# One product of seven made by seven smaller ones, for two sets of output features at a time

## The chip, the core and the metric

The kernel runs on one core of a Trainium2 chip. The core has a matrix engine (TensorE, PE in the profile, with its weight loads as PEld), a vector engine (VectorE, DVE), a scalar engine (ScalarE, ACT), a general engine (GpSimd, POOL) and a queue engine that issues most transfers (SyncE, SP). Each runs its own list of instructions in order, and they wait for one another by semaphores. The metric is the device time of one execution in microseconds (us). Before the change it is 1542.12 us, the median of 3 runs (1541.8 to 1542.74).

## What is computed

One layer for 1024 prompt tokens and 32 sample tokens, together 1056 columns, with 1024 features:

```python
proj = rmsnorm(x, g_mix) @ w_in              # 1024 -> 5120
q, k, v, cb, cc, cx, ga, gc = split(proj)    # 512 each, the gates 1024 each
y_attn = attend(q, k, v) @ w_attn_out
y_conv = (cb * causal_conv(cc * cx)) @ w_conv_out
x = x + (sigmoid(ga) * y_attn + sigmoid(gc) * y_conv) @ w_o
x = x + square(relu(rmsnorm(x, g_ffn) @ w_up)) @ w_down
x = x + sigmoid(rmsnorm(x, g_ple) @ w_ple_gate) * (p @ w_ple)
```

All of it is in fp32. A product of matrices is made in three passes over rounded parts (high by high, high by low, low by high), so each block of weights and activations exists as a high part, rounded by ACT, and a low part, subtracted by DVE.

## The kernel before

Features lie on the partitions, tokens along the columns. The input stage (`w_in`) and the up stage (`w_up`) go set by set: a set is two blocks of 128 output features. `seven` (L206) makes a set by Winograd's form of Strassen's scheme: the set's weights are four quarters (two output blocks by the even and the odd four of the eight blocks of input features), the activations four quarters B11 to B22 (even and odd features by two halves of the tokens), and seven products of sums replace eight. Each product is made in two pieces of 264 columns, and each piece is 12 matmuls (4 blocks of features, three passes). The order on PE is A11·B11, S1·T1, S2·T2, A12·B21, S3·T3, S4·B22, A22·T4, each as piece 0 and piece 1. S2, S3 and A22 add into the same accumulators as A11 (`x`), S4 into that of S1 (`z`), after ACT or DVE has read the earlier sum out (L227 to L256).

PE's list is written by hand. `run` (L268) advances the body of a set by one step, which is mostly one piece, and after it every generator in `side` by one step: `prepare` (L168) makes the weights of the next set (four sums on POOL, then casts on ACT and subtractions on DVE), `fetch_in` and `fetch_up` load the set after it, and `follow` (L575) works on the outputs of the set just made: for q and k a scaling and a split, for v a shift difference `dv` and transposes, for cc, cx and cb the convolution (`conv_in`, L535: scale, multiply, two passes with the taps). `stats_x` (L396) finds the norms of the rows, and PE spreads them by small matmuls over `dg` tiles (L384). So what ACT, DVE and POOL do, and in which order, follows from the step in which it is written.

In the up stage `up_set` applies relu and square on ACT as the sums come out, and `mid_sums` (L1257) makes four sums of halves on DVE for the down stage.

## Time and profile before

| what | us |
|---|---|
| median of 3 runs | 1542.12 |
| the profiled execution | 1543.23 |
| its span, first to last instruction | 1541.5 |
| TensorE busy in the span | 1520.1 |
| VectorE busy | 1061.1 |
| ScalarE busy | 756.8 |
| GpSimd busy | 347.1 |

The busy time of PE is the union of its instructions, which overlap: a matmul is recorded for longer than the distance to the next. What a matmul costs is read from a stretch without gaps, as its length over its count. Waits are listed by the engine that waited and the one that ended the wait.

### The profile page before, as it was taken

The page shows a single profiled execution, that of the slowest core. Times are in us where ns is not written, and L with a number is a line of the kernel's source. Part 1 is how long each engine was busy: PE and PEld are TensorE (multiplying, and loading weights), DVE is VectorE, ACT ScalarE, POOL GpSimd, SP SyncE. Part 2 cuts the span into 40 slices and gives each one's busy share as a digit, 9 for nine tenths or more (in the row PEclk, how much of TensorE's full clock was granted, in tenths as well). Part 3 has the DMA queues.
Part 4 walks back from the last instruction along what each step waited for, and adds up shares of the span by engine and source line. Part 5 has one row for each costly group of instructions (what it writes and reads, how often), then busy time and mean ns, then how long its engine had stood idle before and what let it go on. Part 6 is the DMA issues. An engine that isn't in the chain of part 4 may idle for free.

```text
span 1541.5 us, 29349 instructions
## 1 busy us (share of the span) xinstructions
PE 1520.1 (99%) x11786; PEld 1506.4 (98%) x11786; DVE 1061.1 (69%) x1394; ACT 756.8 (49%) x1384; POOL 347.1 (23%) x294
## 2 busy tenths in 40 slices
PE   8999999999999999999999999999999999999997
PEld 8999999999999999999999999999999999999997
DVE  7534786666688887766677555554586986789856
ACT  6543344443566774333355555555534334444656
POOL 1122332220211105002312222221020221012453
PEclk9999999999999999999999999999999999999999
DMA  6532145544735566235454334434886897583443
GB/s 235 185 123 69 45 178 204 197 146 111 218 108 152 177 220 243 87 125 182 166 184 148 139 141 153 144 136 147 290 305 203 281 327 250 188 283 106 144 132 111
DMA packets 111559, 269.10 MB, mean 175 GB/s; under 512 B 13472, under 2 KB 29216, under 8 KB 111424
## 3 DMA queue, kind: packets, MB, share of 16 engines
q1 hardware_dynamic: 110704, 265.05, 50.9%
q8 instruction: 92, 1.51, 0.4%
q10 hardware_dynamic: 720, 2.19, 0.4%
q14 instruction: 43, 0.35, 0.1%
HBM read 186.46 MB, written 80.73 MB: 173 GB/s over the span
## 4 chain that ended last, share of the span: by engine, by line
PE 92%; DVE 4%; ACT 2%; issue 1%; DMA 0%; SPq 0%; POOL 0%; DVEq 0%; ACTq 0%; POOLq 0%
PE ps_dn L1473 7%; PE ps_dn L1472 7%; PE ps_dn L1474 7%; PE ps_A11u L203 4%; PE ps_A11u L202 4%; PE ps_A11u L204 4%; PE ps_A11i L202 4%; PE ps_A11i L204 4%; PE ps_A11i L203 4%; PE av L874 2%; PE ps_wo L106 2%; PE ps_wo L107 2%; PE ps_wo L108 2%; PE ps_S1u L203 2%; PE ps_S1u L202 2%; PE ps_S1u L204 2%
## 5 line engine op out<-in xcount | busy, mean ns | idle before, releaser
L1473 PE MATMUL ps_dn<-fl,whi_dn 128*128 128x264 f32 x896 | 255.0, 285 | 0.1
L1474 PE MATMUL ps_dn<-fh,wlo_dn 128*128 128x264 f32 x896 | 255.1, 285 | 0.0
L1472 PE MATMUL ps_dn<-fh,whi_dn 128*128 128x264 f32 x896 | 254.9, 285 | 0.0
L1473 PEld LDWEIGHTS ps_dn<-fl,whi_dn 128*128 128x128 f32 x896 | 168.6, 188 | 0.3 <-DVE fl L1381 0.3
L1472 PEld LDWEIGHTS ps_dn<-fh,whi_dn 128*128 128x128 f32 x896 | 168.7, 188 | 0.0
L1474 PEld LDWEIGHTS ps_dn<-fh,wlo_dn 128*128 128x128 f32 x896 | 168.6, 188 | 0.0
L189 POOL TENSOR_TENSOR s_i<-raw_i,raw_i 128x512 f32<-128x512 f32 x30 | 40.5, 1348 | 227.8 <-DVE slS_i L152 206.7
L1365 DVE TENSOR_TENSOR wlo_dn<-raw_dn,whi_dn 128x1024 fp32r<-128x1024 f32 x40 | 71.1, 1778 | 25.1 <-ACT whi_dn L1359 24.4
L819 DVE TENSOR_TENSOR_SCAN r<-r 128x128 f32<-128x128 f32 (+3 forms) x64 | 86.6, 1355 | 2.1 <-POOL r L812 2.1
L1359 ACT CAST whi_dn<-raw_dn 128x1024 fp32r<-128x1024 f32 x40 | 42.0, 1051 | 93.7 <-PE ps_dn L1473 79.5
L189 POOL TENSOR_TENSOR s_u<-raw_u,raw_u 128x512 f32<-128x512 f32 x30 | 44.2, 1473 | 186.1 <-DVE slS_u L152 157.4
L1414 POOL TENSOR_TENSOR c<-c,rs 128x528 f32<-128x528 f32 x16 | 26.7, 1669 | 244.2 <-DVE c L1481 122.7
L1381 DVE TENSOR_TENSOR fl<-mr,fh 128x1056 fp32r<-128x1056 f32 x56 | 69.8, 1248 | 4.6 <-ACT fh L1376 4.6
L152 DVE TENSOR_TENSOR slS_i<-s_i,shS_i 128x512 fp32r<-128x512 f32 x45 | 36.0, 802 | 49.2 <-ACT shS_i L150 49.0
L202 PE MATMUL ps_A11i<-T,shS_i 128*128 128x264 f32 x240 | 68.6, 286 | 0.2 <-ACT u_i L235 0.2
L202 PE MATMUL ps_A11u<-T,shS_u 128*128 128x264 f32 x240 | 68.5, 285 | 0.0
L203 PE MATMUL ps_A11u<-T,shS_u 128*128 128x264 f32 x240 | 68.4, 285 | 0.0
L203 PE MATMUL ps_A11i<-T,shS_i 128*128 128x264 f32 x240 | 68.2, 284 | 0.0
L204 PE MATMUL ps_A11i<-T,slS_i 128*128 128x264 f32 x240 | 68.2, 284 | 0.0
L204 PE MATMUL ps_A11u<-T,slS_u 128*128 128x264 f32 x240 | 68.2, 284 | 0.0
L812 POOL TENSOR_SCALAR_AFFINE_SELECT r<-r 128x128 f32<-128x128 f32 x64 | 26.3, 412 | 166.1 <-ACT r L805 166.0
L1376 ACT CAST fh<-mr 128x1056 fp32r<-128x1056 f32 x56 | 60.1, 1073 | 5.5 <-DMA mr<-mdB 5.5
(462 smaller groups left out, 5594.7 us busy)
## 6 DMA issues: line engine op xcount, KB each, us to landing
raw_dn<-in_w_down_dram SPq DMA_DIRECT2D x56, 512.0 KB, 4.5
raw_i<-in_w_in_dram SPq DMA_DIRECT2D x34, 512.0 KB, 4.4
mr<-mdT SPq DMA_DIRECT2D x32, 528.0 KB, 5.4
raw_u<-in_w_up_dram SPq DMA_DIRECT2D x32, 512.0 KB, 3.6
mdB<-m SPq DMA_DIRECT2D x48, 264.0 KB, 2.5
mr<-mdB SPq DMA_DIRECT2D x24, 528.0 KB, 6.4
s<-gd SPq DMA_DIRECT2D x16, 528.0 KB, 5.4
mdT<-ta SPq DMA_DIRECT2D x32, 264.0 KB, 2.1
```

The lines of the kernel that those rows point to most:

```text
L189: f()
L202: nc.tensor.matmul(p_, wh[:, k, :], o[:, 0, c], start=new and n == 0, stop=False, **on)
L203: nc.tensor.matmul(p_, wh[:, k, :], o[:, 1, c], start=False, stop=False, **on)
L204: nc.tensor.matmul(p_, wl[:, k, :], o[:, 0, c], start=False, stop=z, **on)
L819: nc.vector.tensor_tensor_scan(rev, rev, rev, 1.0, ALU.mult, ALU.bypass)
L1359: nc.scalar.copy(hi, dws[u])
L1365: dve(lo, raw, hi.bitcast(F32), op=sub)
L1376: nc.scalar.copy(h, mraw[v])
L1381: dve(l, mraw.pop(v), opd[v].bitcast(F32), op=sub)
L1472: nc.tensor.matmul(ps, hi[:, j, :], oh, start=j == 0, stop=False)
L1473: nc.tensor.matmul(ps, hi[:, j, :], ol, start=False, stop=False)
L1474: nc.tensor.matmul(ps, lo[:, j, :], oh, start=False, stop=j == NP_ - 1)
```

## The change

From the second normal set of each stage on, sets are made two at a time by `seven_pair`: 14 of the products of a pair are as before, but the two products A12·B21, one of each set, are taken together as one product of a matrix of two sets by the four odd feature blocks, and that is made by the seven-product scheme once more, on quarters. Each of its seven products is 6 matmuls of 264 columns, 42 for the pair in place of 48. The input stage has 7 pairs and the up stage 7, so 84 matmuls fall away. The operands of the inner products are new tiles (`inner_operands`, made once a stage; the inner weights by `prepare_inner` once a pair, with four more sums on POOL). The inner results come together by additions on DVE and copies on ACT. On PE the pieces of a set now follow as A11, S1, S2, S3, S4, and the inner products stand between those of A22. The second set begins with S1, then A11. The weights come in four loads per pair, two of them in two halves, the order of the sets in the input stage is another, and the input rows of `w_in` and `w_up` are stored even blocks first.

```diff
-NBUF = 34
+NBUF = 37
...
+    def prepare_inner(key, odd):
+
+        r = raws[odd]
+        a11, a12, a21, a22 = (r[:, 2 * i : 2 * i + 2, :] for i in range(4))
+        t = wpool[0].tile([P, 4, P], F32, tag="s", name=f"si_{key}", bufs=4)
+        s1, s3 = t[:, 0:2, :], t[:, 2:4, :]
+        his, los = (
+            [wsp.tile([P, KD, P], F32R, tag=f"w{x}", name=f"w{x}{i}_{key}") for i in range(2)] for x in ("hi", "lo")
+        )
+
+        def part(i, c, src):
+            nc.scalar.copy(his[i][:, c, :], src)
+            dve(los[i][:, c, :], src, his[i][:, c, :].bitcast(F32), op=sub)
...
+
+        ws[key] = {"A11": w(0, 0), "A12": w(0, 1), "A22": w(0, 3), "S1": w(1, 0), "S3": w(1, 1), "S2": w(1, 2), "S4": w(1, 3)}
+        part(0, slice(0, 4), r[:, 0:4, :])
+        pool(s1, a21, a22, op=add)
+        yield
+        pool(s3, a11, a21, op=sub)
+        yield
+        pool(a11, s1, a11, op=sub)
+        yield
+        pool(a12, a11, a12, op=sub)
+        yield
+        part(0, slice(6, 8), a22)
+        yield
+        yield
+        part(1, slice(0, 4), t)
+        yield
+        part(1, slice(4, 8), r[:, 0:4, :])
+        yield
...
+    def inner_operands(name, g, load):
+
+        raw = [blk(f"ri{name}{k}", F32, [P, 2, TH]) for k in range(2)]
+        for k in range(2):
+            for i in range(2):
+                load(raw[k][:, i, :], 2 * k + 4 * i + 1)
+        for _ in range(4):
+            yield
+        for k in ("T1", "T2", "T3", "T4"):
+            inner_t[k] = blk(f"yi{k}{name}", F32R, [P, 2, 2, TQ])
+        for k in range(2):
+            g0, g1 = (g[:, 2 * k + i : 2 * k + i + 1] for i in (1, 5))
+            x11, x12, x21, x22 = (raw[k][:, i, j * TQ : j * TQ + TQ] for i in range(2) for j in range(2))
+            nc.scalar.activation(x12, x12, AF.Copy, scale=g0)
+            mix(x22, x22, g1, x12, sub)
+            mix(x12, x11, g0, x12, sub)
+            yield
+            mix(x11, x11, g0, x22, add)
+            mix(x21, x21, g1, x11, sub)
+            yield
+            for n, (kind, src) in enumerate((("T1", x12), ("T2", x11), ("T3", x22), ("T4", x21))):
+                d = inner_t[kind]
+                nc.scalar.copy(d[:, 0, k, :], src)
+                dve(d[:, 1, k, :], src, d[:, 0, k, :].bitcast(F32), op=sub)
+                if n % 2:
+                    yield
...
+    def inner_product(name, w, b, p_=None):
+
+        o = {"B11": low_t[0][0], "B21": low_t[1][0], "B22": low_t[1][1]}.get(b) or inner_t[b]
+        new = p_ is None
+        if new:
+            p_ = group(f"ps_in{name}", TQ)
+        on = dict(skip_group_check=not new)
+        wh, wl = w
+        for k in range(2):
+            nc.tensor.matmul(p_, wh[:, k, :], o[:, 0, k, :], start=new and k == 0, stop=False, **on)
+            nc.tensor.matmul(p_, wh[:, k, :], o[:, 1, k, :], start=False, stop=False, **on)
+            nc.tensor.matmul(p_, wl[:, k, :], o[:, 0, k, :], start=False, stop=k == 1, **on)
+        return p_
...
+    def seven_pair(s0, s1, key, m, last, after=({}, {}), meanwhile=int):
...
+        def middle(i, s5, u2):
+            for t, a, b in q:
+                product(i, "S2", "T2", t, x[t])
+                u2.append(tile_of("u2", t))
+                nc.scalar.copy(u2[t], x[t])
+                yield
+            for t, a, b in q:
+                product(i, "S3", "T3", t, x[t])
+                dve(m(i, 1)[:, b], x[t], s5[t], op=sub)
+                yield
+            done(i, "22")
+            for t, a, b in q:
+                product(i, "S4", "B22", t, z[t])
+                dve(m(i, 0)[:, b], u2[t], z[t], op=sub)
+                yield
+            done(i, "12")
+
+        def end(i, t):
+            product(i, "A22", "T4", t, x[t])
+            last(m(i, 1), q[t][1], x[t])
+
+        p1 = []
+        for t, a, b in q:
+            x[t] = product(0, "A11", "B11", t)
+            p1.append(tile_of("p1", t))
+            nc.scalar.copy(p1[t], x[t])
+            yield
+        s5 = []
+        for t in range(2):
+            s5.append(sums(0, t))
+            yield
+        yield from middle(0, s5, [])
+        xi = inner("A11", "B11")
+        dve(p1[0], xi, p1[0], op=add)
+        zi = inner("S1", "T1")
+        i5 = tile_of("s5", 2)
+        nc.scalar.copy(i5, zi)
+        yield
+        end(0, 0)
+        yield
+        inner("S2", "T2", xi)
+        dve(p1[1], xi, p1[1], op=add)
+        c11 = inner("A12", "B21")
+        dve(m(0, 0)[:, q[0][1]], c11, p1[0], op=add)
+        yield
+        end(0, 1)
+        done(0, "21")
+        meanwhile()
+        yield
+        c = [None, tile_of("p1", 2)]
+        inner("S3", "T3", xi)
+        dve(c[1], xi, i5, op=sub)
+        inner("S4", "B22", zi)
+        dve(m(0, 0)[:, q[1][1]], p1[1], zi, op=sub)
+        done(0, "11")
+        yield
+        s5 = [sums(1, 0)]
+        yield
+        c[0] = tile_of("p1", 3)
+        inner("A22", "T4", xi)
+        nc.scalar.copy(c[0], xi)
+        s5.append(sums(1, 1))
+        yield
+        for t, a, b in q:
+            x[t] = product(1, "A11", "B11", t)
+            dve(m(1, 0)[:, a], x[t], c[t], op=add)
+            yield
+        done(1, "11")
+        yield from middle(1, s5, [])
+        for t in range(2):
+            end(1, t)
+            yield
+            if t == 0:
+                done(1, "near")
+        done(1, "21")
+        for k in (s0, s1, key):
+            ws.pop(k)
...
+    def ahead_of(nm, a, n):
+
+        return after(n, prepare(f"{nm}{a}", (5, 7, 9, 11, 13, 15), (f"{nm}{a}e", f"{nm}{a}o", 0)))
+
+    def pair_side(nm, a, b, then=None):
+
+        order = ("S1", "A11", "S2", "S3", "S4", "A22")
+        side.append(prepare_inner(f"{nm}{a}y", f"{nm}{a}o"))
+        side.append(after(4, prepare(f"{nm}{b}", (4, 6, 8, 11, 14, 16), (f"{nm}{a}e", f"{nm}{a}o", 1), order)))
+        if then:
+            for n, f in zip((6, 9, 11, 21), pair_loads(nm, *then)):
+                side.append(after(n, call(f)))
+            side.append(ahead_of(nm, then[1], 17))
 
...
-    SETS = [("g", n) for n in range(0, EARLY_GATES, 2)] + [(nm, 0) for nm in ("cc", "cx", "cb", "q", "k", "v")]
-    SETS += [(nm, 2) for nm in ("q", "k", "v", "cc", "cx", "cb")]
+    SETS = [("g", n) for n in range(0, EARLY_GATES, 2)]
+    SETS[4:4] = [("k", 0)]
+    SETS += [("v", 0), ("cc", 0), ("cx", 0), ("cb", 0), ("k", 2), ("q", 0), ("v", 2), ("cc", 2), ("cx", 2), ("q", 2), ("cb", 2)]
...
+-            if s_ + 1 < len(SETS):
-                side.append(prepare(f"i{s_ + 1}", AT_IN))
...
-            if s_ + 2 < len(SETS):
-                side.append(after(5, call(fetch_in, s_ + 2)))
-            m = blk(f"m1_i{s_}"), blk(f"m2_i{s_}")
-            run(seven(f"i{s_}", *m, copy_of))
-            follow(nm, n, m)
+            more = a + 2 < len(SETS)
+            pair_side("i", a, a + 1, in_pair(a + 2, a + 3) if more else None)
...
+            run(input_pair(a, a + 1))
...
-            run(up_set(s_))
...
+        for a in range(2, NSET, 2):
+            more = a + 2 < NSET
+            pair_side("u", a, a + 1, up_source(a + 2, a + 3) if more else None)
...
+            run(up_pair(a, a + 1))
```

Place one is TensorE in the up stage, sixth set: the end of S2·T2 (piece 1 into `ps_A11u6_1`) and what follows. Before:

```order
L202 MATMUL ps_A11u6_1_10962<-T2_3_9410,shS2_u6_10871 128x264
L203 MATMUL ps_A11u6_1_10962<-T2_3_9410,shS2_u6_10871 128x264
L204 MATMUL ps_A11u6_1_10962<-T2_3_9410,slS2_u6_10873 128x264
L202 MATMUL ps_A12u6_0_11041<-B21_0_8708,whi_u6_10804 128x264
L203 MATMUL ps_A12u6_0_11041<-B21_0_8708,whi_u6_10804 128x264
L204 MATMUL ps_A12u6_0_11041<-B21_0_8708,wlo_u6_10805 128x264
```

Now:

```order
L311 MATMUL ps_A11u6_1_11184<-T2_3_9574,shS2_u6_11153 128x264
L312 MATMUL ps_A11u6_1_11184<-T2_3_9574,shS2_u6_11153 128x264
L313 MATMUL ps_A11u6_1_11184<-T2_3_9574,slS2_u6_11155 128x264
L311 MATMUL ps_A11u6_0_11161<-T3_0_9761,shS3_u6_11199 128x264
L312 MATMUL ps_A11u6_0_11161<-T3_0_9761,shS3_u6_11199 128x264
L313 MATMUL ps_A11u6_0_11161<-T3_0_9761,slS3_u6_11201 128x264
```

S3 goes into `ps_A11u6_0`, which S2's piece 0 filled one piece earlier; before, both pieces of A12·B21 came in between.

Place two is VectorE in the input stage, in the set (before) or pair (now) that follows cx, where `conv_in` works on cx's second block (`m2_i6` before, `m2_i8` now). Before:

```order
L152 TENSOR_TENSOR slA22_i7_2093<-raw_i7_1_1637,shA22_i7_2091 128x512
L141 SCALAR_TENSOR_TENSOR m1_i6_1757<-m1_i5_1524,vecT_78,m1_i6_1757 128x1054
L141 SCALAR_TENSOR_TENSOR m1_i6_1757<-ce0_2053,vecT_78,cs0_2054 128x2
L98 TENSOR_TENSOR wlo_i8_2098<-raw_i8_0_1868,whi_i8_2097 128x1024
L238 TENSOR_TENSOR m1_i7_1990<-ps_A12i7_0_2118,p1_i70_1992 128x264
L482 TENSOR_TENSOR m2_i6_1758<-m2_i6_1758,rs_120 128x1056
L238 TENSOR_TENSOR m1_i7_1990<-ps_A12i7_1_2133,p1_i71_1993 128x264
L541 TENSOR_TENSOR m2_i5_1525<-m2_i5_1525,m2_i6_1758 128x1056
L243 TENSOR_TENSOR m2_i7_1991<-ps_A11i7_0_1998,s5_i70_1996 128x264
```

Now:

```order
L726 TENSOR_TENSOR m2_i8_2541<-m2_i8_2541,rs_120 128x1056
L237 TENSOR_TENSOR wlo1_i9y_2642<-si_i9y_2638,whi1_i9y_2640 128x512
L400 TENSOR_TENSOR m2_i9_2767<-ps_A11i9_1_2646,s5_i91_2704 128x264
L785 TENSOR_TENSOR m2_i7_2236<-m2_i7_2236,m2_i8_2541 128x1056
L237 TENSOR_TENSOR wlo1_i9y_2642<-raw_i9o_2291,whi1_i9y_2640 128x512
L405 TENSOR_TENSOR m1_i9_2804<-u2_i90_2726,ps_S1i9_0_2667 128x264
L166 TENSOR_TENSOR slS1_i10_2816<-raw_i10r_2543,shS1_i10_2814 128x512
L405 TENSOR_TENSOR m1_i9_2804<-u2_i91_2748,ps_S1i9_1_2691 128x264
L155 SCALAR_TENSOR_TENSOR m2_i8_2541<-m2_i7_2236,vecT_78,m2_i8_2541 128x1055
L799 TENSOR_SCALAR cs1_2809<-ce1_2808,vecT_78 128x2
L155 SCALAR_TENSOR_TENSOR cs1_2809<-ce1_2808,vecT_78,cs1_2809 128x2
L425 TENSOR_TENSOR p1_i90_2635<-ps_inA11i9y_2837,p1_i90_2635 128x264
```

The inner weights' low part `wlo1_i9y`, which the second inner product reads, and the addition into `p1_i90`, which frees the accumulator of the inner products, stand behind the scaling (L726), the multiplication (L785) and the first tap pass (L155).

Place three is VectorE where the row norms are spread (`dg`, nine tiles, the first shown), three steps into a set or pair. Before:

```order
L248 TENSOR_TENSOR m1_i2_757<-u2_i21_762,ps_S1i2_1_832 128x264
L152 TENSOR_TENSOR slS3_i3_1006<-s3_i3_790,shS3_i3_1004 128x512
L409 RECIPROCAL rst_122<-rst_122 128x9
L152 TENSOR_TENSOR slS4_i3_1048<-s4_i3_791,shS4_i3_1046 128x512
L391 TENSOR_SCALAR dg_1101<-ident_69,rst_122 128x128
L391 TENSOR_SCALAR dg_1104<-ident_69,rst_122 128x128
```

Now:

```order
L166 TENSOR_TENSOR slS2_i3_1024<-s2_i3_863,shS2_i3_1022 128x512
L155 SCALAR_TENSOR_TENSOR rix0_951<-rix0_951,vecT_78 128x264 x2
L653 RECIPROCAL rst_122<-rst_122 128x9
L155 SCALAR_TENSOR_TENSOR rix0_951<-rix0_951,vecT_78 128x264 x2
L237 TENSOR_TENSOR wlo0_i3y_1056<-raw_i3o_790,whi0_i3y_1054 128x512
L166 TENSOR_TENSOR slS3_i3_1078<-s3_i3_864,shS3_i3_1076 128x512
L283 TENSOR_TENSOR yiT1x_1026<-rix0_951,yiT1x_1026 128x264
L283 TENSOR_TENSOR yiT2x_1027<-rix0_951,yiT2x_1027 128x264
L283 TENSOR_TENSOR yiT3x_1028<-rix0_951,yiT3x_1028 128x264
L283 TENSOR_TENSOR yiT4x_1029<-rix0_951,yiT4x_1029 128x264
L635 TENSOR_SCALAR dg_1122<-ident_69,rst_122 128x128
```

Between the weights' low parts and the first `dg` now stand the four sums for the inner operands (`rix0`, twice two), one low part of inner weights and four low parts of inner operands.

## The prediction

> **What bounds the kernel now.** I read the page's first part, then its chain of work that ended last, then two stretches of the stages that change.

> ```profile
> span 1541.5 us, 29349 instructions
> PE 1520.1 (99%) x11786; PEld 1506.4 (98%) x11786; DVE 1061.1 (69%) x1394; ACT 756.8 (49%) x1384; POOL 347.1 (23%) x294
> PE 92%; DVE 4%; ACT 2%; issue 1%; DMA 0%; SPq 0%; POOL 0%; DVEq 0%; ACTq 0%; POOLq 0%
> 56.40:374.00 317.60, 315.86 (x2588) 314.31 (x2587) 194.55 (x275) 140.03 (x308) 85.53 (x60) 1.00 0.41 140
> 790.00:1098.50 308.50, 308.50 (x2530) 307.87 (x2529) 175.15 (x260) 169.61 (x323) 76.84 (x56) 1.00 0.43 152
> L202 PE MATMUL ps_A11u<-T,shS_u 128*128 128x264 f32 x240 | 68.5, 285 | 0.0
> PE ps_g L202 <- ACT B L328: 6.1, 1, 6.1
> PE ps_S1i L202 <- ACT shS_i L150: 0.6, 1, 0.6
> ```

> TensorE (PE) has 99% of the span and 92% of the chain. The two stretches are the input stage and the up stage: length and sum, then busy time and count of PE, its weight loads, VectorE (DVE), ScalarE (ACT) and GpSimd (POOL), then the granted clock, 1.00. In the up stage PE has no gap at all. A matmul is recorded for 285 ns, but they overlap: 308.50 / 2530 = 0.122 us is the price of one. A piece (12 matmuls) is then 1.46 us and an inner product (6) 0.73. DVE is busy 61% and 57% there, ACT 44% and 55%, so on average both have room. What matters is when their results are due. In the set scheme waits are small: 0.6 us in one wait for the weights of S1; the 6.1 us are at the program's start.

> The execution profiled took 1543.23 us, 1.1 above the median of 1542.12. I sum against the former and take 1.1 off at the end.

> **The change, part by part.**

> *Removed work.* 84 matmuls of 264 columns at 0.122: -10.2 us. PE is the bound in both stages, so this is on the path as long as PE isn't made to wait.

> *The shorter slack.* S2 fills the accumulator into which S3 adds. In between it must be read out.

> ```profile
> 861.78 0.28 PE L204 MATMUL ps_A11u<-T,slS_u 128*128 128x264 f32 x1
> 861.90 0.28 PE L202 MATMUL ps_A12u<-B,whi_u 128*128 128x264 f32 x1
> 862.10 0.38 ACT L235 COPY u_u<-ps_A11u 128x264 f32<-128x264 f32 x1 [0.56 <-PE ps_A11u L204]
> 883.99 0.43 DVE L238 TENSOR_TENSOR m<-ps_A12u,p_u 128x264 f32<-128x264 f32 x1 [1.28 <-PE ps_A12u L204]
> ```

> The copy starts 0.2 us after PE's next product (861.90) and takes 0.38: it is done 0.58 after the piece ends; for a DVE addition 0.2 + 0.43. Before, three pieces (4.4 us) lay between S2 piece 0 and S3 piece 0, so ACT could come 3.8 us late for nothing. Now one piece does, 1.46, and it may be late by 0.88. The same holds for S2 after A11 in the second set of a pair, and the inner accumulators are refilled after about two pieces. Lateness of ACT and DVE that cost nothing now stops PE, and I go through the places where they are late.

> *cx, pairs (9,10) and (15,16) of the input stage.* At their start DVE makes the convolution of the cx set just ended: per block a scaling, a multiplication, two tap passes and three small operations.

> ```profile
> 176.01 1.25 DVE L482 TENSOR_TENSOR m_i<-m_i,rs 128x1056 f32<-128x1056 f32 x1
> 177.52 1.25 DVE L541 TENSOR_TENSOR m_i<-m_i,m_i 128x1056 f32<-128x1056 f32 x1
> 178.87 1.18 ACT L549 ACTIVATE m_i<-m_i,vecT 128x1056 f32<-128x1056 f32 x1 [5.59 <-DVE m_i L541]
> L141 DVE SCALAR_TENSOR_TENSOR m_i<-m_i,vecT,m_i 128x1055 f32<-128x1055 f32 x4 | 5.3, 1315 | 2.5 <-ACT m_i L549 2.5
> L555 DVE TENSOR_SCALAR cs<-ce,vecT 128x2 f32<-128x2 f32 x4 | 0.9, 225 | 0.0
> L152 DVE TENSOR_TENSOR slS_i<-raw_i,shS_i 128x512 fp32r<-128x512 f32 x15 | 10.3, 684 | 1.8 <-ACT shS_i L150 1.8
> L150 ACT CAST shS_i<-raw_i 128x512 fp32r<-128x512 f32 x15 | 9.4, 626 | 0.0
> L551 ACT COPY ce<-vecT 128x1 f32<-128x1 f32 x8 | 1.1, 180 | 0.0
> 178.90:199.30 20.40, 20.17 (x163) 19.75 (x163) 18.51 (x20) 9.61 (x20) 6.69 (x4) 1.00 0.12 42
> ```

> The last row is such a set before: DVE is busy 18.51 of 20.40 us and PE loses 0.23. Now, in DVE's row order, from the pair's start on PE: 1.20 for ACT's copy (0.58) and cast (0.62), low part 0.68, scaling 1.25, inner low part 0.68, a wait of 0.3, low part 0.68, multiplication 1.25, so to 6.06. Then ACT scales the product by a tap (1.18), makes three small copies (0.54), a copy 0.38 and the cast for S4 0.62: to 8.80, and DVE waits for it. DVE's next: low part 0.68, tap 1.32, two small ones 0.45, tap 1.32, small 0.22, half a low part (256 columns, estimated a little over half of 0.68) 0.36, low part 0.68, addition 0.43, and of the second block scaling 1.25, inner low part 0.68, addition 0.43, multiplication 1.25, inner low part 0.68: to 18.5. Addition 0.43; the low part for the next set waits on ACT behind the second tap scaling (1.18 + 0.54 + 0.62 after 17.9) until 20.2; 0.68, addition 0.43, tap 1.32, small 0.45, and then the addition into p1 (0.43) ends at 23.5. That one frees the inner accumulator for the inner S2. PE is there after ten pieces, two inner products and one piece: 14.6 + 1.46 + 1.46 = 17.6. So PE waits 5.9 us; of this 0.6 already at the inner S1. Nothing hides that; PE's list is in order. Floor 5.9, since every operation has its undisturbed price. Ceiling 8.5: two of the 1.25 us operations meet POOL.

> ```profile
> 871.12 1.29 POOL L189 TENSOR_TENSOR s_u<-raw_u,raw_u 128x512 f32<-128x512 f32 x1 [11.30 <-DVE slS_u L152]
> 874.47 1.62 POOL L189 TENSOR_TENSOR s_u<-raw_u,raw_u 128x512 f32<-128x512 f32 x1 [0.69 <-DVE slS_u L152]
> 874.98 1.68 DVE L1263 TENSOR_TENSOR m<-m,m 128x528 f32<-128x528 f32 x1
> 876.70 0.71 DVE L1265 TENSOR_TENSOR ta<-m 128x528 f32<-128x528 f32 x1
> ```

> Such a sum on DVE takes 0.71, and 1.68 while POOL works, so a meeting costs up to POOL's 1.29. I take half a meeting: 6.5 for each of the two pairs, 13.0. [...]

> *v, pairs (7,8) and (13,14).* PE transposes the shift difference `dv`, and DVE makes it behind the low part of S4.

> ```profile
> L511 DVE TENSOR_TENSOR dv<-m_i x4: 1218/1708/2203, 249.8 to 326.7; 128x1023 f32<-128x1023 f32 x4
> PE pt_v L525 <- DVE dv L511: 0.5, 2, 0.3
> ```

> ACT reaches the cast for S4 after the copy of S1's piece 1 (5.85 + 0.58 + 0.62 = 7.05); low part to 7.7; dv in 1.22 to 2.20: 8.9 to 9.9. PE is at the transposes after five pieces, 7.4. That is 1.5 to 2.5. The second block's dv follows the addition into p1 (19.0) and is done at 20.2 to 21.2, PE, so delayed, comes at 19.8: 0.4 to 1.3. Floor 2.0 a pair, ceiling 3.8; with dv's mean, 2.5: 5.0 for both. Before, these waits were 0.5 us in all.

> *Row norms, pair (3,4).* PE spreads them from nine `dg` tiles.

> ```profile
> L391 DVE TENSOR_SCALAR dg<-ident,rst x9: 276/286/1314, 82.4 to 86.0; 128x128 f32<-128x128 f32 x9
> L392 PE MATMUL pr<-dg,ones x18: 195/275/377, 84.7 to 86.7; 128*128 128x128 f32 x16, 128*128 128x32 f32 x2
> L141 DVE SCALAR_TENSOR_TENSOR B<-x,vecT,B 128x264 fp32r<-128x264 f32 x16 | 6.7, 490 | 0.0
> ```

> Ahead of them DVE now has four sums for the inner operands (4 x 0.49), an inner low part 0.68 and four low parts of 264 columns (a little over half of 0.68, 0.36 each): 4.1 us. The first dg was ready at 82.7, 2.0 ahead of PE's 84.7; the last ones came as PE used them. So 4.1 - 2.0 = 2.1 at least, 4.1 at the end of the row, with two meetings with POOL 6.7. I take 3.2.

> *The other starts and middles.* Taking the first two lines of slack: in each of the 14 pairs S2 piece 0 of the second set adds onto A11, read by a DVE addition at 0.63 after the piece, due at 1.46: 0.8 to spare, where before there were 3.8. One meeting with POOL costs 1.29 - 0.8 = 0.5; half of the pairs: 0.25 each, 3.5. Floor 0 (PE cannot gain here), ceiling 1.29 each, 18.

> *Loads.* Six transfers a pair in place of four, of the same bytes.

> ```profile
> raw_i<-in_w_in_dram SPq DMA_DIRECT2D x34, 512.0 KB, 4.4
> raw_u<-in_w_up_dram SPq DMA_DIRECT2D x32, 512.0 KB, 3.6
> ```

> They land 4.4 and 3.6 us after issue. The last halves are asked for at about 25 of a pair's 40.3 us (330 x 0.122) and are cast at the next pair's start: 10 us cover them. Nothing. If SP fell behind by more than 10 us, each further one would be a PE wait.

> *POOL.* 56 more sums (by the change's own list), 4 a pair; at 1.29 (half of that for 256 columns) it stays at a quarter of the stages, so its price is only in the meetings above. *New DVE and ACT work* (127 and 81 instructions, some 0.4 to 0.7 each) has the idle 40% to go into, apart from the places named.

> The sum: -10.2 + 13.0 + 5.0 + 3.2 + 3.5 = +14.5, so 1557.7 by the profiled execution, 1556.6 by the median. With all floors (18 of waits) it is +7.8, with all ceilings (50) +40.

> **The rivals.**

> *Faster: the lateness doesn't reach PE.* It is one mechanism: DVE and ACT do the cx and v work in the time that their idle shares leave, for instance because waits I added one after another overlap. For it: DVE 39% idle, and in the cx window above PE lost 0.23 though DVE was at 91%. Against it: that window had 4.4 us of slack and now has 1.46. It decides if all the waits that I count, 24.7 us, come under 10.2; with none of them the time is 1532, with half 1544.

> *Locks everywhere.* Each pair meets POOL in its middle and the tap passes are held too: 18 in place of 3.5, 17 in place of 13: 1557 + 18.5 = 1575, up to 1582. Speaking for it: POOL's 56 sums more, near the places with the least to spare. Against it: POOL is busy 27% and 25% of the two stretches.

> *The clock falls in the waits.* In the profile the granted clock is 1.00 in both stretches and the 6.1 us wait at the start left no mark on the row. [...]

> *No change.* The waits come to 10 us by chance, as the middle between floor and rival: 1542.

> **How the numbers follow.** My forecast, 1557, has 0.61, its own range 1547 (a floor missed by 4) to 1572. Faster has 0.20, locks everywhere 0.08, the clock 0.03, no change 0.08. About 0.2% (3 us) is what measuring this kernel can tell from no change. So slower 0.61 + 0.08 + 0.03 = 0.72, same 0.08, faster 0.20. The range from 1534 to 1573 leaves out the gain in full and the locks at their worst.

> **What would show it.** In the profile after, PE should have 84 matmuls fewer and gaps in the input stage: at the inner S2 of (9,10) and (15,16), ended by DVE's addition into p1, some 6 us each; at the transposes of dv, 1.5 to 2.5 us; at the first row-norm matmuls 2 to 4 us. The up stage, which has no such followers, should be shorter by 3 to 5 us and show only small waits. I am wrong if PE's waits for DVE stay under 10 us in total, if the up stage carries the loss, or if the chain there passes through DMA or POOL.

## The result, and the profile after

The changed kernel takes 1585.74 us (median of 4 runs, 1584.45 to 1586.98) against 1542.43 before: a ratio of 1.0281, 95% interval 1.0263 to 1.0299. It is slower by 43, and I had forecast 1557 with 1573 as the upper end. The sign was right and the size was not: in the profiled spans the difference is 43.8 us (1585.3 against 1541.5), and even the sum with all ceilings gave only 40.

The page of the changed kernel, its first part, and its chain:

```profile
span 1585.3 us, 29521 instructions
PE 1527.9 (96%) x11702; PEld 1511.1 (95%) x11702; DVE 1133.4 (71%) x1530; ACT 775.2 (49%) x1466; POOL 406.2 (26%) x350
PE 77%; DVE 8%; ACT 2%; issue 2%; DMA 1%; SPq 0%; POOL 0%; DVEq 0%; ACTq 0%; POOLq 0%
```

PE has 84 instructions fewer (11786 to 11702), as it should, and yet it is busy 7.8 us longer. Two things are to be explained: time in which PE stands, and time in which it works and is slow. DVE is busy 72 us more for 136 instructions more.

Stretch by stretch, input stage and up stage, after and then before (columns as in the prediction):

```profile
56.60:409.40 352.80, 322.17 (x2535) 318.92 (x2534) 230.91 (x344) 149.80 (x347) 115.30 (x86) 0.96 0.37 129
826.40:1140.10 313.70, 308.97 (x2486) 306.76 (x2485) 208.48 (x323) 176.05 (x359) 99.97 (x82) 0.99 0.43 152
```

```profile
56.40:372.80 316.40, 314.66 (x2578) 313.11 (x2577) 193.38 (x273) 139.65 (x307) 84.68 (x59) 1.00 0.40 139
790.00:1098.40 308.40, 308.40 (x2529) 307.77 (x2528) 175.05 (x260) 169.51 (x323) 76.84 (x56) 1.00 0.43 152
```

The input stage is longer by 36.4 us, the up stage by 5.3, what follows it by 2.1 (1585.3 - 1140.1 against 1541.5 - 1098.4); the stretch between the stages is the same. The last column but two is the granted clock: 0.96 and 0.99, where it was 1.00.

PE's waits after:

```profile
PE pt_v L769 <- DVE dv L755: 7.1, 2, 3.6
PE ps_g L311 <- ACT B L572: 6.1, 1, 6.1
PE pr L636 <- DVE dg L635: 5.9, 1, 5.9
PE ps_inA11i9y L296 <- DVE p_i L425: 4.5, 1, 4.5
PE ps_inA11i15y L296 <- DVE p_i L425: 4.5, 1, 4.5
PE ps_inA11u2y L296 <- DVE p_u L425: 2.9, 1, 2.9
PE ps_A11i L311 <- DVE m_i L457: 2.5, 2, 2.1
PE ps_inS1i15y L298 <- DVE wlo_i15y L237: 1.7, 1, 1.7
PE ps_inS1i9y L298 <- DVE wlo_i9y L237: 1.7, 1, 1.7
...
PE ps_dn L1779 <- DVE fl L1687: 1.3, 1, 1.3
...
PE ps_inS1u2y L298 <- DVE wlo_u2y L237: 1.0, 1, 1.0
```

The places are those of the forecast: dv, dg, and the additions into p1 in pairs (9,10) and (15,16). Not forecast is the first up pair (`u2y`, 3.9 us) and the start of the down stage. But all waits of this list together do not make the difference. The rest shows in the stretches that the profile gives at half clock:

```profile
88.48:95.31 6.83, 4.43 (x20) 4.44 (x21) 4.36 (x10) 1.30 (x4) 2.18 (x2) 0.50 0.00 0
180.64:187.47 6.83, 5.83 (x27) 5.87 (x28) 3.15 (x6) 2.46 (x7) 1.98 (x1) 0.50 0.20 77
242.08:248.91 6.83, 5.04 (x23) 5.07 (x24) 5.03 (x10) 0.20 (x1) 0.01 (x1) 0.50 0.46 109
324.00:327.41 3.41, 3.39 (x16) 3.41 (x17) 1.28 (x3) 1.15 (x3) 1.00 (x1) 0.50 0.17 68
385.44:388.85 3.41, 3.41 (x18) 3.41 (x17) 2.87 (x6) 0.00 (x0) 0.00 (x0) 0.50 0.39 114
870.14:876.97 6.83, 6.13 (x28) 6.16 (x29) 6.04 (x10) 2.72 (x8) 1.79 (x2) 0.50 0.29 102
```

After each of the six longest waits but the one at the program's start, PE runs at 0.50 for 3.41 or 6.83 us, also when it has work: 28.2 us of PE's work at half clock. What that costs shows in the distance between matmuls. Early in the kernel before, these two pairs of rows stand 0.5 us apart:

```profile
12.18 0.42 PE L203 MATMUL ps_g<-B,whi_i 128*128 128x264 f32 x1
12.40 0.42 PE L204 MATMUL ps_g<-B,wlo_i 128*128 128x264 f32 x1
...
12.92 0.28 PE L204 MATMUL ps_g<-B,wlo_i 128*128 128x264 f32 x1
13.04 0.28 PE L202 MATMUL ps_g<-B,whi_i 128*128 128x264 f32 x1
```

Slow matmuls of 264 columns start 0.22 us apart and fast ones 0.12, and 0.22 is also the distance inside the six stretches. So half clock does not double the price of 0.122: of each 0.22 us 0.098 is lost, 45%, and summed over the six stretches 12.7 us. PE is busy 7.8 longer in spite of 10.2 less work, which makes 18.0; 5.3 of that is not attributed in full. Part of it is that a matmul is recorded for 0.285 us where the next one normally starts after 0.122, so 0.16 us ahead of every wait counts as busy and stands in no wait of the list.

How DVE came to be so late is seen ahead of the row norms. GpSimd's rows there, then DVE's, and then DVE's at one of the cx places:

```profile
84.59 1.04 POOL L248 TENSOR_TENSOR raw_i3o<-si_i3y,raw_i3o 128x256 f32<-128x256 f32 x1 [13.09 <-DVE wlo_i3y L237]
85.71 0.79 POOL L250 TENSOR_TENSOR raw_i3o<-raw_i3o 128x256 f32<-128x256 f32 x1
86.47 1.45 POOL L222 TENSOR_TENSOR s_i<-raw_i3e,raw_i4r 128x512 f32<-128x512 f32 x1
87.99 1.33 POOL L222 TENSOR_TENSOR raw_i4r<-raw_i4r 128x512 f32<-128x512 f32 x1
89.41 1.33 POOL L222 TENSOR_TENSOR s_i<-raw_i4r,raw_i3e 128x512 f32<-128x512 f32 x1
```

```profile
84.96 0.95 DVE L283 TENSOR_TENSOR yiT1x<-rix,yiT1x 128x264 fp32r<-128x264 f32 x1
85.84 0.95 DVE L283 TENSOR_TENSOR yiT2x<-rix,yiT2x 128x264 fp32r<-128x264 f32 x1
86.72 1.49 DVE L283 TENSOR_TENSOR yiT3x<-rix,yiT3x 128x264 fp32r<-128x264 f32 x1
88.13 1.49 DVE L283 TENSOR_TENSOR yiT4x<-rix,yiT4x 128x264 fp32r<-128x264 f32 x1
89.54 1.28 DVE L635 TENSOR_SCALAR dg<-ident,rst 128x128 f32<-128x128 f32 x1
...
228.82 2.35 DVE L155 SCALAR_TENSOR_TENSOR m_i<-m_i,vecT,m_i 128x1055 f32<-128x1055 f32 x1
231.09 1.25 DVE L799 TENSOR_SCALAR cs<-ce,vecT 128x2 f32<-128x2 f32 x1
```

These subtractions of 264 columns take 0.43 where GpSimd rests (a row of the next section); here five sums of GpSimd run one behind the other from 84.59 to 90.74, the first released when DVE finished the inner weights' low part (L237), and each of the five DVE operations ends 0.1 to 0.3 us after the sum that runs beside it. A tap pass takes 2.35 (1.32 before) and an operation on two columns 1.25 (0.22 before), beside two sums of GpSimd that run from 228.43 to 230.06 and from 230.13 to 232.31.

### The profile page after: what moved, and what is told of

It reads as the page before. It is cut to its first block, busy times and chain, and to the rows that moved or that the text cites. A ratio compares the mean times of both kernels' runs of the same rounds, so it can differ in the third digit from the quotient of the medians.

```text
span 1585.3 us, 29521 instructions
## 1 busy us (share of the span) xinstructions
PE 1527.9 (96%) x11702; PEld 1511.1 (95%) x11702; DVE 1133.4 (71%) x1530; ACT 775.2 (49%) x1466; POOL 406.2 (26%) x350
## 4 chain that ended last, share of the span: by engine, by line
PE 77%; DVE 8%; ACT 2%; issue 2%; DMA 1%; SPq 0%; POOL 0%; DVEq 0%; ACTq 0%; POOLq 0%
PE ps_dn L1780 7%; PE ps_dn L1778 7%; PE ps_dn L1779 7%; PE ps_A11u L311 3%; PE ps_A11u L312 3%; PE ps_A11u L313 3%; PE ps_A11i L311 2%; PE ps_A11i L312 2%; PE ps_A11i L313 2%; PE av L1149 2%; PE ps_wo L106 2%; PE ps_wo L107 2%; PE ps_wo L108 2%; PE pa L1130 2%; PE ps_pg L106 2%
## 5 line engine op out<-in xcount | busy, mean ns | idle before, releaser
L1720 POOL TENSOR_TENSOR c<-c,ssq 128x528 f32<-128x528 f32 x16 | 26.7, 1668 | 241.9 <-DVE c L1787 122.4
L311 PE MATMUL ps_A11i<-T,shS_i 128*128 128x264 f32 x240 | 71.0, 296 | 3.3 <-DVE m_i L457 2.5
L166 DVE TENSOR_TENSOR slS_i<-s_i,shS_i 128x512 fp32r<-128x512 f32 x45 | 40.8, 906 | 44.3 <-ACT shS_i L164 44.0
L312 PE MATMUL ps_A11i<-T,shS_i 128*128 128x264 f32 x240 | 69.7, 290 | 0.0
L312 PE MATMUL ps_A11u<-T,shS_u 128*128 128x264 f32 x240 | 68.5, 285 | 0.0
L1533 ACT ACTIVATE m<-m 128x528 f32<-128x528 f32 x45 | 29.1, 647 | 75.9 <-DVE m L400 30.4
L1134 DVE TENSOR_TENSOR at<-pa,at 128x512 fp32r<-128x512 f32 (+2 forms) x96 | 51.0, 550 | 16.1 <-ACT at L1133 15.3
## 6 DMA issues: line engine op xcount, KB each, us to landing
raw_dn<-in_w_down_dram SPq DMA_DIRECT2D x56, 512.0 KB, 4.6
raw_pg<-in_w_ple_gate_dram SPq DMA_DIRECT2D x15, 512.0 KB, 3.5
```

What stands on the lines that cost most here:

```text
L311: nc.tensor.matmul(p_, wh[:, k, :], h, start=new and n == 0, stop=False, **on)
L312: nc.tensor.matmul(p_, wh[:, k, :], l, start=False, stop=False, **on)
L1134: nc.vector.tensor_tensor(al, pt[:, :nb, :], ah.bitcast(F32), op=ALU.subtract)
```

## The experiments

The theory after the result: (1) PE waits at the places of the forecast, and longer than an undisturbed DVE would make it wait, because GpSimd's sums hold DVE up; (2) every wait that leaves some 3.4 us nearly without work costs again, by half clock. The rivals: DVE has simply too much work, and the clock is a mark of the wait without a price.

**GpSimd's sums left out, in the changed kernel and in the one before.** In `prepare` and `prepare_inner`:

```diff
-        s2, s3, s4 = (wpool[0].tile([P, 4, P], F32, tag="s", ...
+        s2, s3, s4 = a11, a21, a22
...
-        pool(s1, a21, a22, op=add)
```

> Left out: all sums of weights on GpSimd in the sets and pairs of both stages; the casts read the raw weights in their place, so the outputs are others. Everything else, with the order on each engine, stays. Theory 1 (DVE operations with two SBUF inputs stand still while a GpSimd sum runs, and that makes PE's waits long): the dg wait falls from 5.9 to 2.0-2.8, the two dv waits from 3.5 to 1.5-2.0 each, the two cx places from 6.2 to 3-4.5 each, the second up set's pair from 3.9 to under 1.5; waits under about 2.5 us no longer bring the clock down, so at most two drops are left: 1555 to 1563 in all. Theory 2 (DVE has simply too much of its own work at these places): every wait within 0.5 us of the changed kernel's, six drops, 1580 or more.

> The kernel before with GpSimd's sums of weights left out in both stages, as in the run that left them out of the changed kernel; the casts read raw weights, so the outputs are others. Theory 1 (before, the slack of three pieces hid the sums and what they hold up): 1540 to 1543, within 0.2% of the kernel before, so that the sums cost the changed kernel 32 us and the old one nothing. Theory 2 (the sums cost both kernels): under 1535.

Measured: 1553.68 us for the changed kernel without the sums (ratio to before 1.0072, 1.0057 to 1.0087), and 1542.30 for the one before without them (0.9999, 0.9990 to 1.0008). So the same sums cost the kernel before nothing and the changed one 32 us, although DVE is busy less without them in both (1020.5 against 1061.1 us in the kernel before). Of the changed kernel without them: busy times, the up stage, PE's waits, and one of DVE's rows ahead of dg:

```profile
PE 1514.9 (98%) x11702; PEld 1500.8 (97%) x11702; DVE 1065.4 (69%) x1530; ACT 775.7 (50%) x1466; POOL 174.5 (11%) x174
...
801.40:1105.60 304.20, 304.20 (x2486) 303.34 (x2485) 180.23 (x323) 176.12 (x359) 0.00 (x0) 1.00 0.45 158
...
PE ps_inA11i15y L286 <- DVE p_i L415: 4.1, 1, 4.1
PE ps_inA11i9y L286 <- DVE p_i L415: 4.1, 1, 4.1
PE pt_v L759 <- DVE dv L745: 2.7, 2, 1.4
...
PE pr L626 <- DVE dg L625: 1.7, 1, 1.7
...
84.37 0.43 DVE L273 TENSOR_TENSOR yiT1x<-rix,yiT1x 128x264 fp32r<-128x264 f32 x1
```

DVE has the same 1530 instructions and is busy 68 us less: by so much its operations lasted longer beside the sums. That the casts could have been late by waiting for the sums is not borne out: in the changed kernel no wait of ACT for a weight's cast is ended by GpSimd. dg went from 5.9 to 1.7, dv from 7.1 to 2.7, the first up pair's waits are gone, and the up stage takes 304.2 us: 4.2 less than before, most of the 5.1 that 42 matmuls are worth. The cx places went from 6.2 to 4.1 each only: two thirds of that wait is DVE's and ACT's own work in line. Two stretches of half clock are left, behind those two. Theory 1 holds for all places but cx, where both hold; the total is 1.3 below its range.

**PE kept busy in the waits.** Matmuls with a matrix of zeros ahead of the six longest waits:

```diff
+    def filler(p_, n, start):
+        for i in range(n):
+            nc.tensor.matmul(p_, zero, view("B11", ...), start=start and i == 0, stop=i == n - 1, ...)
...
         def end(i, t):
             product(i, "A22", "T4", t, x[t])
+            if (i, t) == (0, 0) and key in fills:
+                filler(x[t], fills[key], False)
```

> At the six longest waits of PE stand matmuls with a matrix of zeros (40 ahead of the row norms, 20 ahead of each of the two first dv transposes, 24 behind A22 piece 0 of pairs (9,10) and (15,16), 16 in the first up pair); they run while PE would wait and add nothing. Theory 1 (each wait that leaves a stretch of 3.4 us nearly idle brings 3.4 to 6.8 us at half clock): waits plus fillers together as long as the waits before, no stretch of the profile at half clock, 1571 to 1575, so 11 to 14 us under the changed kernel. Theory 2 (the clock only mirrors the waits and costs nothing by itself): 1584 to 1588, or more by the fillers.

Measured: 1579.65 us, 6.1 less than the changed kernel, half of what theory 1 gave and outside what theory 2 gave. The six stretches at half clock are gone, but a new one came, behind this wait that was 2.1 at most:

```profile
PE ps_A11i L319 <- DVE m_i L469: 4.1, 2, 3.8
```

PE, no longer slowed, met DVE again where it was still late. This wait, the 3.41 us at half clock behind it (1.5 us lost) and 1.8 us in place of 0.5 at the same additions in the up stage take back some 4.4 us. So the 12.7 us are not all to be had: part of the half clock lies over DVE's catching up.

**A wait made in the kernel before.** There DVE is not late elsewhere, so the price of the half clock stands alone.

```diff
+    def hold(n):
+        t = cpool.tile([P, P], F32, tag="dg", name="dg", bufs=4)
+        nc.vector.memset(t, 1.0)
+        for _ in range(6 * n):
+            dve(t, t, t, op=ALU.mult)
...
+        hold(6)
         for q0 in (0, 3, 6):
             spread(rst, rs, q0)
```

In the second run `hold` stands ahead of the four dv instead, with 2, 1, 2 and 1.

> The kernel before, with 36 multiplications of a 128x128 tile by itself on DVE ahead of the first dg tile (some 7 us, less the 2.0 that dg was early), so that PE waits once, 5 to 6 us, at the row norms. Theory 1 (a stretch of 3.4 us nearly without PE work brings half clock for 3.4 to 6.8 us, and this costs PE half of it): the time rises by the wait and 1.7 to 3.4 us more, to 1549 to 1552. Theory 2 (the half clock costs nothing of its own): the time rises by the wait alone, within 0.7.

> The kernel before, with the same 36 multiplications spread: 12, 6, 12 and 6 ahead of the four dv. PE waits four times, 1 to 2.6 us each. Both theories: no stretch at half clock, and the time rises by the sum of the four waits, 5 to 8 us, within 0.7. Told apart from the run with one wait by the time beyond the wait.

Measured: 1555.80 with one wait, 1558.33 with four; in both the multiplications took longer than I had set (DVE's 35 operations in the first wait took 9.81 us), so the waits were longer than expected. The wait in the first, the waits in the second, and the stretches at half clock of both:

```profile
PE pr L399 <- DVE dg L398: 10.9, 1, 10.9
86.99:100.64 13.65, 5.26 (x24) 5.26 (x25) 9.53 (x34) 1.36 (x3) 0.00 (x0) 0.50 0.00 0
```

```profile
PE pt_v L533 <- DVE dv L519: 10.6, 4, 3.0
255.03:261.86 6.83, 6.11 (x28) 6.14 (x29) 3.90 (x7) 3.06 (x7) 0.00 (x0) 0.50 0.48 172
272.09:275.50 3.41, 3.25 (x15) 3.28 (x16) 1.81 (x5) 0.75 (x2) 2.55 (x2) 0.50 0.11 44
330.12:333.53 3.41, 3.41 (x18) 3.41 (x17) 2.45 (x4) 2.06 (x4) 0.00 (x0) 0.50 0.78 269
```

One wait of 10.9 us cost 13.2: the wait and 45% of 5.26. Four waits of 10.6 together (10.1 more than before) cost 15.7 by the median: the waits and 45% of the 12.8 us that PE worked at 0.50 (the profiled execution itself was the slowest of the four runs, 1559.09). The half clock has a price of its own, and the rival falls. My expectation for the four was wrong: behind three of the four waits, the longest of which was 3.0 us, the clock comes down too. Here four shorter waits cost more than one long one, since three of them paid again.

**The up stage alone.** The input stage set by set as before.

> The input stage goes set by set in the order of before, only the up stage has pairs. Theory 1 (the input stage lost 36.6 of the 43.8 us, the up stage 5.4, by waits of their own): 1547 to 1551, with the first up pair's waits (2.9 and 1.0) and one drop of the clock. Theory 2 (the up stage's waits come from what the input stage left late): the up stage shorter than before by 4 to 5 us, 1537 to 1539.

Measured: 1549.07 us (ratio 1.0042, 1.0026 to 1.0059). The up stage took 312.0 us (308.4 before) with its own waits (2.9, 1.0, and 1.9 at the additions L458, this kernel's place for L457), so the up stage's loss does not come from the input stage. Outside it PE waits longer too: 2.2 for dv in place of 0.5, and 2.6 at the down stage's start. Here the waits of the first pair brought no half clock, where one drop was expected.

**The late places moved, in three runs.** First the row norms, dv and the second cx block:

```diff
-        for _ in range(3):
+        for _ in range(12):
             yield
...
+            yield
+            yield
             w = min(3 * P, T - q0 * P)
...
-        side.extend([gens[0], after({"v": 7, "cx": 6}.get(nm, 1), gens[1])])
+        side.extend([gens[0], after({"v": 9, "cx": 13, "cb": 5}.get(nm, 1), gens[1])])
```

> Same work as the changed kernel, moved in three places: the row norms 9 steps later with two steps between the dg tiles and the matmuls on them; two more steps between dv and its transposes; the second cx block 7 steps later and the second cb block 4 steps later. Theory 1 (the waits are places where DVE is late, not DVE as a whole): the dg and dv waits under 0.5 us each, the cx places under 2.5 each, at most two drops of the clock left, 1549 to 1557. Theory 2 (DVE's share in the input stage is too high, so that what is moved is missed elsewhere): new waits for DVE of the same total, 1570 or more.

Measured: 1573.97 us. PE waits no more for dg, 1.3 for dv in place of 7.1, and 1.0 at each cx place in place of 6.2; but it waits 8.5 for the additions L457 in place of 2.5, up to 4.3 at once, and 4.4 in place of 1.2 at the start of the stage that follows (`pa`). 12 us were won where 29 to 37 were expected. Theory 2 is nearer. Then also S1 piece 1 of second sets behind A11, the cx blocks and the first cb block two steps further (the second cb block back where the change has it), and inner operands and the down stage's loads earlier:

```diff
-        s5.append(sums(1, 1))
-        yield
         for t, a, b in q:
...
         done(1, "11")
+        s5.append(sums(1, 1))
+        yield
```

> The whole change with all moves: row norms later, dv two steps ahead of its transposes, the second cx block 9 steps later and the second cb block 6, S1 piece 1 behind A11 in second sets, inner operands earlier in both stages, the down stage's first loads earlier. Theory 1: each move removes its own wait, 1543 to 1555, and no half clock. Theory 2 (what is moved is missed elsewhere): 1560 or more.

Measured: 1563.54 us (ratio 1.0138). Theory 2's range holds, and three stretches at half clock are left. Now PE waits 9.7 us for ACT's copies of S2 (`u`, L396) in the input stage, 4.8 at once. ACT's rows ahead of that copy:

```profile
265.17 1.08 ACT L825 CAST cvh<-m_i 128x1056 fp32r<-128x1056 f32 x1
...
270.54 1.04 ACT L747 CAST kh<-m_i 128x1024 fp32r<-128x1024 f32 x1 [4.28 <-DMA cvd<-cvh]
...
271.61 0.37 ACT L396 COPY u_i<-ps_A11i 128x264 f32<-128x264 f32 x1
```

The moved cb block is stored so late that k's cast, which takes the buffer (`cvh`) that this transfer reads, waits 4.28 us for it to land, and the copy that PE needs stands behind that cast: a new kind of wait in place of the one removed. And with cx and cb left where the change has them:

> Both stages in pairs; moved are the row norms (9 steps later, dg two steps ahead), dv (two steps ahead), S1 piece 1 of second sets, mid_sums (6 steps later), the up stage's inner operands and the down stage's first loads (4 steps earlier); the cx and cb blocks stay where the change has them. Theory 1 (the places are independent): only the two cx places keep their 6.2 us each with a drop of the clock each, 1549 to 1557. Theory 2 (what is moved is missed elsewhere in the input stage): 1560 or more.

Measured: 1572.02 us. The cx places kept 6.2 each with half clock for 6.83 us each, as theory 1 said; but this kernel has mid_sums 6 steps later, and that made a new wait of 9.2 us in the up stage (see below). Of the remaining miss, some 6 us, most are waits at four places: 1.7, 1.1 and 1.1 in the middle of pairs (3,4), (7,8) and (13,14), and 1.3 at dv. In the input stage no order that I tried has room for the cx work; whether one exists stays open.

**A version of the up stage that gains.** The up stage in pairs, the input stage not, with S1 piece 1 behind A11, the inner operands 4 steps earlier, and the down stage's first loads 4 steps earlier:

> Pairs in the up stage only, with three moves: in the second set of a pair S1 piece 1 stands behind A11 and not ahead of it, so the additions that S2 waits for have two pieces and not one; the inner operands of the up stage are made 4 steps earlier, ahead of the first pair; the down stage's first loads and splits 4 steps earlier. Theory 1 (the up stage's 9 us of waits are these two places, and the down stage's start another 2.5): 1539 to 1543. Theory 2 (DVE stays late through GpSimd's sums, and the next place waits): 1545 to 1549.

Measured: 1543.31 us, ratio 1.0004 (0.9996 to 1.0013): no change. Waits of 0.4 to 1.1 us in each pair remained at the additions that S2 needs; ahead of them on DVE stand the four sums of `mid_sums` for the first set of the pair. These moved by 6 steps, and dv one step ahead of its transposes:

```diff
-                side.append(mid_sums(s_, m(0), m(1)))
+                side.append(after(6, mid_sums(s_, m(0), m(1))))
```

> The up stage in pairs with the three moves of the run before, and two more: mid_sums of a pair's first set begin 6 steps later, behind the additions that S2 of the second set waits for; dv one step earlier against its transposes in the input stage (which goes set by set). Theory 1 (the 4.2 us left at these additions in the up stage are the four sums ahead of them on DVE): they fall under 1, dv's waits under 0.5, 1537 to 1540.5. Theory 2 (DVE is late there by GpSimd's sums in any case): 1541 to 1544.

Measured: 1547.27 us, worse, and above both ranges. The same sums now stand ahead of the subtractions that A22 waits for:

```profile
PE ps_A11u L312 <- DVE m L401: 9.1, 7, 1.6
```

So by 3 steps, between the two:

> As the run before of the up stage in pairs, but mid_sums begin 3 steps later and not 6: behind the second of the additions that S2 waits for, and four steps ahead of the subtractions that A22 waits for. Theory 1 (one place where four sums of DVE fit in, between the two): PE's waits in the up stage's pairs after the first under 1 us together, 1537 to 1540, faster than both kernels. Theory 2 (no such place): waits of 4 us or more stay, 1542 or more.

Measured: 1536.81 us, ratio 0.9966 (0.9954 to 0.9978): faster than both kernels. The up stage and what follows it:

```profile
788.60:1093.20 304.60, 304.13 (x2486) 303.31 (x2485) 202.31 (x324) 175.94 (x360) 99.50 (x82) 1.00 0.45 158
1093.20:1534.40 441.20, 432.35 (x3372) 431.48 (x3370) 343.25 (x412) 203.75 (x288) 104.28 (x70) 1.00 0.65 216
```

3.8 us of the gain are the pairs (308.4 to 304.6, of 5.1 possible). 1.9 come after the up stage (443.1 to 441.2); which edit brings them is not shown. The earlier loads and the dv step do not need the pairs; they were not tried alone.

## Why the prediction was wrong

**Two steps failed.** The first is the price of meeting GpSimd: the sum took a meeting as a matter of chance (half a meeting at each cx place, half of the pairs at the other starts), and what the sums really cost, with the half clock that the longer waits brought, is 32 us, by the run without them. The second is the clock: I gave that rival 0.03, and in the sum the half clock was nothing. It cost 12.7 us of nominal time. I had argued that the wait of 6.1 us at the program's start "left no mark on the row". The row was of a later stretch. The matmuls right behind that wait start 0.22 us apart until 12.6 us and 0.12 after that, as the rows of the kernel before show: PE was slow there, although the clock column reads 1.00 for that stretch too. So the wait was no evidence for a clock that holds through a wait. I had no number for the half clock from any run. In the changed kernel it came in stretches of 3.41 or 6.83 us, at a loss of 45% of PE's work time in them, and a window need not be idle to bring one. The stretches start whole multiples of 3.413 us apart; by windows of that length counted from the first of them, past the program's start, the full clock fell after each of the seven in which PE was busy 1.21 us or less (ahead of the six stretches, and once at the program's end), and after none with 1.62 or more.

**The terms of the sum**, forecast and measured:

| term | forecast | measured |
|---|---|---|
| 84 matmuls | -10.2 | -10.2 |
| cx, two pairs | 13.0 | 12.4 |
| dv, two pairs | 5.0 | 7.1 |
| dg | 3.2 | 5.9 |
| other starts and middles | 3.5 | 15.9, by difference |
| half clock | 0 | 12.7 |
| sum | 14.5 | 43.8 |

- *Removed work.* Right: without the sums, the up stage got 4.2 of its 5.1 us.
- *cx.* The place, the order (0.6 forecast at the inner S1, 1.7 measured, then the addition into p1) and the size were right. My floor of 5.9 was not a floor: with GpSimd's sums left out it is 4.1. I took the engines' own work in line for 5.9 and GpSimd's part for 0.6, where the runs give 4.1 and 2.1; that the two errors nearly cancel is luck.
- *dv and dg.* The places were right. Undisturbed they are 1.35 each and 1.7, near my floors (1.5 for the first dv, 2.1). The measured 3.5 and 5.9 are near my ceilings. I took about one meeting for dg, and for dv only the spread of its own duration, at places where GpSimd's sums come one behind the other; at dg there are five, the first released by a DVE operation just ahead: not chance but order. The wait that I forecast for the second block's dv did not come, since PE came later there.
- *Other starts and middles.* 3.5 stands against 15.9: 3.0 at the additions L457, 3.9 in the first up pair (inner operands are made there too, which I had counted only in the input stage), and 2.7 at the down stage's start. The remaining 6.3 lie in short waits and in what a wait costs beyond its listed length; they are not shown one by one. I forecast the up stage shorter by 3 to 5; it is longer by 5.3.
- *The tap passes.* The sum had no term for their meetings with GpSimd, since none met it in the trace before; only the rival "locks everywhere" took them as held up, without a row for it. Rows of the changed kernel show it: 2.35 for 1.32.
- *The rivals.* "Locks everywhere" (GpSimd's sums hold DVE up in every pair; 1575 to 1582, 0.08) and "the clock falls" (0.03) came both, and the first brought the second: without the sums four of the six stretches at half clock are gone. I had counted them as alternatives. The faster rival, that lateness does not reach PE, holds for nothing in the input stage and for the up stage only after three moves.

## What to carry to other kernels

When an edit shortens the distance between a producer on PE and its reader on another engine, list what that reader's engine has in its row at that moment, and what GpSimd starts at the same moment: lateness that was free is then paid. Count a wait of PE over some 2 us with a surcharge, since in the changed kernel, past its start, each window of 3.41 us with 1.21 us of work or less (so 2.2 us or more without) was followed by 3.41 us or more at half clock; two causes that lengthen the same wait are not alternatives. Moving the late work helped here only where a gap of its length lies between two deadlines, as `mid_sums` showed at 0, 3 and 6 steps.
